# Scaling the memory rows of a two-layer decoder: four VectorE multiplications behind two powers, or four on GpSimd behind one

## The chip, the cores and the metric

The kernel runs on one core of one Trainium2 chip. The core has engines that run side by side, each with a queue of its own that it works off in order: TensorE (PE in the profile) multiplies matrices and transposes, VectorE (DVE), ScalarE (ACT) and GpSimd (POOL) do elementwise work, SyncE (SP) starts most transfers. An instruction starts when the one ahead of it on its engine is through and what it waits for is there. The metric is the device time of one execution in microseconds (us), the median of the runs; before the change 1529.76 us (three runs, 1529.23 to 1529.96).

## The reference, cut to what matters

```python
for l in range(DEPTH):                                   # 2 layers
    a = hybrid_mixer(rms_norm(x, pre_mix_g[l]), ...)     # latent + dilated attention
    x = x + rms_norm(a, post_mix_g[l])
    c = memory_cross_attention(rms_norm(x, pre_xattn_g[l]), rms_norm(mem, mem_g[l]), ...)
    x = x + rms_norm(c, post_xattn_g[l])
    x = x + rms_norm(squared_relu_mlp(rms_norm(x, pre_mlp_g[l])), post_mlp_g[l])

def rms_norm(x, g):
    return x * rsqrt(mean(x * x, axis=-1) + 1e-6) * g
```

x is 512 tokens by 1024, mem 256 memory tokens by 1024, all in float32. The change is in `rms_norm(mem, ...)`: the factor of each memory row, and the multiplication by it. The gain g is taken into the weights w_xk and w_xv.

## The kernel before

Products in float32 accuracy are made of three fast passes (lines 247 to 249): every operand is split into a rounded high part, by ScalarE (`whi`, `mth`), and a rest, by VectorE (`wlo`, `mtl`). PSUM, where TensorE writes, is cut into small pools of buffers: the pool `pst` has two buffers (tag "t") for everything that is transposed, the pool `pss` two (tag "s") for attention scores. A third tile of a pool has to wait until the first has been read out.

In the mixer, attention over 16 heads (`attention`, 8 dilated and 8 latent ones) is the main strand. `weave` fills in the latent projections (`latent`) and the keys and values of the memory (`memory`). With the 31st step of `latent`, `memory_norm` (line 829) is let in, one step of it for each step of `latent`: it loads the four 128x512 pieces of the memory (`mr`, two tiles t of 128 tokens by two halves n), takes sums of squares on ScalarE (line 381), then for each t adds the halves' sums (line 385, `nmm`), takes the power -0.5 on GpSimd (line 139, `nmr`) and multiplies the rows on VectorE (line 841). `memory` then transposes the scaled rows on TensorE (`tp<-ident,mr`, line 230), and ScalarE and VectorE split the transposed tile into `mth` and `mtl` (lines 203 and 205), from which the keys (`pfm<-mtl,whi`) are computed.

The same stretch of the program holds, of the attention: scores of latent heads (`sp<-ring`, line 481), their bias and maximum on VectorE (line 486), the exponential on ScalarE (line 490), the row factors (line 494, VectorE) and the multiplication by them on GpSimd (line 497), transposes of the probabilities (`ptp`, line 230) and their copies out of PSUM (`PT`, line 514 on VectorE, line 516 on ScalarE), and the weighted values (`op`, line 238); of the latent projections: query columns (`ptm`, then `qst`, line 767), rotary parts on GpSimd (lines 620 to 624), transposed queries (`qtp`) and keys (`pkn`), both split into `ring`, and the shared rotary key copied by GpSimd (line 802).

The order of the instructions on each engine isn't written out by hand here. A scheduler takes the program in the order in which the generators yield it, with its own idea of what is ready when, and lays out each engine's queue. So an edit of a few instructions moves others nearby.

Of the kernel before, what the change touches and what calls it, by code (L numbers as in the profile page):

```python
# [16 lines left out]
OP = mybir.AluOpType  # L17
# [15 lines left out]
EPS = 1e-6  # L33
# [12 lines left out]
def block_kernel(ctx: ExitStack, tc, x, mem, positions, rel_bias, w_in, q_norm_g, w_uq, kv_norm_g,  # L46
# [3 lines left out]
    nc = tc.nc  # L50
# [13 lines left out]
    def unit(name, shape=(128, 512), dt=F32):  # L64
        return un.tile(list(shape), dt, tag="u", name=name)

    def small(name, w):
        return sm.tile([128, 4], F32, tag="sm", name=name)[:, :w]
# [68 lines left out]
    def rpow(m, name):  # L137
        r = small(name + "r", m.shape[1])
        nc.gpsimd.tensor_tensor(r, m, mhalf[:, :m.shape[1]], op=OP.pow)
        return r  # L140
# [236 lines left out]
    def sumsq(src, ss, scale=1.0, junk=None):  # L377
        w = src.shape[-1]
        if junk is None:
            junk = unit("junk", (128, w))  # L380
        nc.scalar.activation(junk, src, AF.Square, scale=scale, accum_out=ss)

    def row_rstd(ms, tag):
        m = small(tag + "m", 1)
        nc.vector.scalar_tensor_tensor(m, ms[0], EPS, ms[1], op0=OP.add, op1=OP.add)
        return rpow(m, tag)
# [198 lines left out]
    for l in range(DEPTH):  # L585
# [241 lines left out]
        mr = [[None, None], [None, None]]  # L827

        def memory_norm():
            for t in range(2):  # L830
                for n in range(2):
                    mr[t][n] = unit("mr")
                    nc.sync.dma_start(mr[t][n], mem[0, t * 128:(t + 1) * 128, n * 512:(n + 1) * 512])
            yield
            for t in range(2):
                ms = small("mms", 2)
                for n in range(2):
                    sumsq(mr[t][n], ms[:, n:n + 1], scale=1.0 / 32.0)
                r = row_rstd((ms[:, 0:1], ms[:, 1:2]), "nm")
                for n in range(2):  # L840
                    nc.vector.tensor_scalar(mr[t][n], mr[t][n], r[:, 0:1], None, op0=OP.mult)
                yield

        def memory():
# [17 lines left out]
            for n in range(2):  # L862
                def ev_vx(t, ps, n=n):
# [6 lines left out]
                                           if SPLIT else None, 2, ev_vx, whole=True)  # L870

        latent_gen = with_at(latent(), memory_norm(), MEM_AT)
        outs = []

# [379 lines left out]
```

## Time and profile before

| what | value |
|---|---|
| median of 3 runs | 1529.76 us |
| profiled execution, its own time | 1530.0 us |
| its span, first to last instruction | 1528.2 us |
| PE busy | 1500.1 us, 98% |
| DVE busy | 981.5 us, 64% |
| ACT busy | 819.9 us, 54% |
| POOL busy | 251.0 us, 16% |
| mean granted TensorE clock | 0.994 |

The profile lists, for each engine, how long it was busy and with what. An idle time carries in brackets the instruction that ended it. Busy shares are means over the whole span; the change touches two stretches of some 37 us, one in each layer, and there the shares differ. Starts of instructions on one engine, one after the other, give the time from step to step; a listed duration reaches past the start of the next, since instructions overlap in the pipeline.

### The profile page before, as it was taken

The numbers are of one execution on the slowest core, as the hardware profiler recorded it, in microseconds if no ns is written. First come the engines' busy times: TensorE is split into PE (matmuls) and PEld (weight loads), VectorE is DVE, ScalarE is ACT, GpSimd is POOL, SyncE is SP. The second block draws the span as 40 slices with busy tenths as digits, with TensorE's granted clock in tenths as the row PEclk, the third lists the DMA queues.
The fourth block names the chain that finished last, engine by engine and source line by source line (L and its number), as shares of the span: only waits on it lengthen the run. The fifth ranks groups of instructions, "written<-read, shape, count | busy, mean of one in ns | idle before, by whom it ended". The sixth has DMA issues, their size and how long they took to land.

```text
span 1528.2 us, 21224 instructions
## 1 busy us (share of the span) xinstructions
PE 1500.1 (98%) x7861; PEld 1260.7 (82%) x7861; DVE 981.5 (64%) x1701; ACT 819.9 (54%) x1578; POOL 251.0 (16%) x438
## 2 busy tenths in 40 slices
PE   8999999999999999999999999999999999999997
PEld 6787788898898888888878877878988988888886
DVE  5556865456458668594874666654554694958668
ACT  5366755355356364554654666744454654546363
POOL 2143721021020000000011445201111100000002
PEclk9999999999999999999999999999999999999999
DMA  6423223513131505153642331253322324060535
GB/s 237 154 83 104 83 84 109 181 56 124 56 111 56 179 28 179 42 162 100 209 127 64 118 110 57 70 175 119 107 83 69 122 69 154 15 193 27 182 82 124
DMA packets 89580, 168.28 MB, mean 110 GB/s; under 512 B 6358, under 2 KB 12164, under 8 KB 89476
## 3 DMA queue, kind: packets, MB, share of 16 engines
q1 hardware_dynamic: 86436, 161.15, 32.7%
q0 software_dynamic: 2752, 5.24, 2.1%
q8 instruction: 62, 1.02, 0.3%
q10 hardware_dynamic: 288, 0.52, 0.1%
q14 instruction: 42, 0.34, 0.1%
HBM read 158.49 MB, written 11.03 MB: 111 GB/s over the span
## 4 chain that ended last, share of the span: by engine, by line
PE 83%; DVE 9%; issue 3%; ACT 2%; POOL 1%; DMA 1%; SPq 0%; DVEq 0%; POOLq 0%; ACTq 0%
PE pfm L248 12%; PE pfm L247 12%; PE pfm L249 12%; PE ptm L247 6%; PE ptm L249 6%; PE ptm L248 6%; PE sp L481 3%; PE wa L247 3%; PE wa L249 3%; PE wa L248 3%; PE op L238 3%; DVE wlo L199 3%; PE ptp L230 2%; PE wc L249 1%; PE wc L247 1%
## 5 line engine op out<-in xcount | busy, mean ns | idle before, releaser
L248 PE MATMUL pfm<-xth,wlo 128*128 128x512 f32 (+1 forms) x896 | 322.4, 360 | 0.6
L247 PE MATMUL pfm<-xtl,whi 128*128 128x512 f32 (+1 forms) x896 | 322.2, 360 | 0.0
L249 PE MATMUL pfm<-xth,whi 128*128 128x512 f32 (+1 forms) x896 | 321.6, 359 | 0.0
L199 DVE SCALAR_TENSOR_TENSOR wlo<-raw,gT,whi 128x512 fp32r<-128x512 f32 (+3 forms) x332 | 231.6, 735 | 126.0 <-ACT whi L193 123.7
L193 ACT ACTIVATE whi<-raw,gT 128x512 fp32r<-128x512 f32 (+2 forms) x324 | 209.5, 697 | 173.0 <-PE pfm L249 87.3
L248 PEld LDWEIGHTS pfm<-xth,wlo 128*128 128x128 f32 x896 | 169.2, 189 | 27.2 <-DVE wlo L199 1.6
L249 PEld LDWEIGHTS pfm<-xth,whi 128*128 128x128 f32 x896 | 169.2, 189 | 25.4 <-issue 0.5
L247 PEld LDWEIGHTS pfm<-xtl,whi 128*128 128x128 f32 x896 | 169.2, 189 | 24.8
L164 ACT ACTIVATE whi<-raw 128x1024 fp32r<-128x1024 f32 x112 | 118.2, 1060 | 130.7 <-PE pfm L249 54.1
L165 DVE TENSOR_TENSOR wlo<-raw,whi 128x1024 fp32r<-128x1024 f32 x112 | 134.9, 1221 | 39.2 <-ACT whi L164 39.2
L1075 POOL DMA_DIRECT2D raw<-in_w_down x8 | 9.8, 1230 | 596.2 <-DVE raw L1078 540.1
L247 PE MATMUL wa<-wlo,fh 128*128 128x512 f32 x240 | 93.6, 390 | 0.5 <-DVE acc L1184 0.5
L248 PE MATMUL wa<-whi,fl 128*128 128x512 f32 x240 | 93.4, 389 | 0.0
L249 PE MATMUL wa<-whi,fh 128*128 128x512 f32 x240 | 93.4, 389 | 0.0
L497 POOL TENSOR_SCALAR P<-P,rs 128x128 f32<-128x128 f32 (+3 forms) x128 | 72.3, 580 | 124.7 <-DVE rs L494 109.1
L490 ACT ACTIVATE P<-P,nm 128x128 f32<-128x128 f32 (+3 forms) x128 | 71.2, 557 | 23.9 <-DVE nm L486 23.5
L185 DVE TENSOR_TENSOR wlo<-raw,whi 128x1024 fp32r<-128x1024 f32 x32 | 39.1, 1223 | 59.4 <-ACT whi L184 58.6
L247 PE MATMUL ptm<-wlo,xth 128*128 128x512 f32 (+2 forms) x192 | 68.5, 358 | 2.6 <-DVE wlo L199 1.7
L184 ACT ACTIVATE whi<-raw 128x1024 fp32r<-128x1024 f32 x32 | 33.9, 1061 | 67.3 <-PE ptm L249 60.2
L1078 DVE TENSOR_TENSOR raw<-raw 128x1024 f32<-128x1024 f32 x56 | 68.0, 1220 | 0.2
L248 PE MATMUL ptm<-whi,xtl 128*128 128x512 f32 (+2 forms) x192 | 67.0, 349 | 0.6 <-DVE xtl L205 0.6
L249 PE MATMUL ptm<-whi,xth 128*128 128x512 f32 (+2 forms) x192 | 66.3, 347 | 0.0
(257 smaller groups left out, 3241.6 us busy)
## 6 DMA issues: line engine op xcount, KB each, us to landing
raw<-in_w_up SPq DMA_DIRECT2D x64, 512.0 KB, 4.8
raw<-in_w_down SPq DMA_DIRECT2D x64, 512.0 KB, 4.3
raw<-in_w_in SPq DMA_DIRECT2D x24, 512.0 KB, 5.5
raw<-in_w_xk SPq DMA_DIRECT2D x16, 512.0 KB, 4.8
raw<-in_w_xv SPq DMA_DIRECT2D x16, 512.0 KB, 4.0
raw<-in_w_mix_out SPq DMA_DIRECT2D x16, 512.0 KB, 4.4
raw<-in_w_xq SPq DMA_DIRECT2D x16, 512.0 KB, 6.5
raw<-in_w_xo SPq DMA_DIRECT2D x16, 512.0 KB, 3.6
```

Source lines behind the costliest of these rows:

```text
L164: nc.scalar.activation(hi, raw, AF.Copy)
L165: nc.vector.tensor_sub(lo, raw, hi.bitcast(F32))
L193: weight_parts[:] = [nc.scalar.activation(cols(hi, k, False), cols(raw, k, True), AF.Copy, scale=g).ins]
L199: nc.vector.scalar_tensor_tensor(lv, rv, g, hv, op0=OP.mult, op1=OP.subtract)
L238: nc.tensor.matmul(ps, lhsT=lhsT, rhs=rhs, start=start, stop=stop)
L247: in_order(nc.tensor.matmul(ps, lhsT=lh, rhs=rl, start=first, stop=False, skip_group_check=more))
L248: in_order(nc.tensor.matmul(ps, lhsT=ll, rhs=rh, start=False, stop=False, skip_group_check=more))
L249: in_order(nc.tensor.matmul(ps, lhsT=lh, rhs=rh, start=False, stop=last, skip_group_check=more))
L481: in_order(nc.tensor.matmul(sp[:, :L], lhsT=q[:, i * 128:(i + 1) * 128], rhs=k[:, :L], start=n == 0, stop=n == len(parts) - 1))
L490: nc.scalar.activation(Pi, Pi, AF.Exp, bias=nm[:, i:i + 1], scale=-1.0, accum_out=rs[:, i:i + 1])
L497: nc.gpsimd.tensor_scalar(Pq, Pq, rs[:, q:q + 1], 1.0, op0=OP.mult, op1=OP.mult)
L1078: nc.vector.tensor_add(tile_, tile_, more)
```

## The change

The two tiles share one `nmm` of two columns and one power of two columns. The sums of squares of both come first, in two steps of `memory_norm`, the multiplications after them, in two more, on GpSimd in place of VectorE. The memory's loads stay as they are, and no transfer is moved on SyncE's queue.

```diff
             yield
+            ms = small("mms", 4)
             for t in range(2):
-                ms = small("mms", 2)
                 for n in range(2):
-                    sumsq(mr[t][n], ms[:, n:n + 1], scale=1.0 / 32.0)
-                r = row_rstd((ms[:, 0:1], ms[:, 1:2]), "nm")
+                    sumsq(mr[t][n], ms[:, 2 * n + t:2 * n + t + 1], scale=1.0 / 32.0)
+                yield
+            m = small("nmm", 2)
+            nc.vector.scalar_tensor_tensor(m, ms[:, 0:2], EPS, ms[:, 2:4], op0=OP.add, op1=OP.add)
+            r = rpow(m, "nm")
+            for t in range(2):
                 for n in range(2):
-                    nc.vector.tensor_scalar(mr[t][n], mr[t][n], r[:, 0:1], None, op0=OP.mult)
+                    nc.gpsimd.tensor_scalar(mr[t][n], mr[t][n], r[:, t:t + 1], 1.0, op0=OP.mult, op1=OP.mult)
                 yield
```

The scheduler lays out the queues anew around it, in each layer in the same way. On TensorE, the scores of the first latent head over 384 and 512 keys (`sp`) stood inside the weighted values (`op`) before:

```order
L230 MATMUL ptp<-ident,P 128x128 x6
L238 MATMUL op<-PT,vd 64x512
L238 MATMUL op<-PT,vd 64x384
L481 MATMUL sp<-ring 128x384 x3
L481 MATMUL sp<-ring 128x512 x3
L238 MATMUL op<-PT,vd 64x384
L238 MATMUL op<-PT,vd 64x256 x2
L238 MATMUL op<-PT,vd 64x128 x2
L248 MATMUL ptm<-whi,cl 128x384
```

Now these scores are issued right behind the transposed queries, some twenty instructions earlier, and the same place reads:

```order
L230 MATMUL ptp<-ident,P 128x128 x3
L249 MATMUL ptm<-whi,ch 128x384
L230 MATMUL ptp<-ident,P 128x128 x3
L238 MATMUL op<-PT,vd 64x512
L238 MATMUL op<-PT,vd 64x384 x2
L238 MATMUL op<-PT,vd 64x256 x2
L238 MATMUL op<-PT,vd 64x128 x2
L247 MATMUL ptm<-wlo,ch 128x384
```

So the seven remaining products of the weighted values stand together. Some thirty instructions later on TensorE, behind the keys of the latent heads (`pkn`), the next scores, the transposes of the probabilities (`ptp`) and those of the second memory tile follow. Before:

```order
L249 MATMUL pkn<-ch,whi 128x512
L481 MATMUL sp<-ring 128x128 x3
L230 MATMUL ptp<-ident,P 128x128 x4
L481 MATMUL sp<-ring 128x256 x3
L230 MATMUL ptp<-ident,P 128x128 x6
L230 MATMUL tp<-ident,mr 128x128 x8
L481 MATMUL sp<-ring 128x384 x3
L481 MATMUL sp<-ring 128x512 x2
L247 MATMUL pfm<-mtl,whi 128x256
```

Now the ten transposes of the probabilities come in one piece. The last six of them are two tiles of three; they changed places, so that the first three now take the PSUM buffer that the first four have filled and that ScalarE copies out (line 516):

```order
L249 MATMUL pkn<-ch,whi 128x512
L481 MATMUL sp<-ring 128x128 x3
L481 MATMUL sp<-ring 128x256 x3
L230 MATMUL ptp<-ident,P 128x128 x10
L230 MATMUL tp<-ident,mr 128x128 x8
L481 MATMUL sp<-ring 128x384 x3
L481 MATMUL sp<-ring 128x512
L247 MATMUL pfm<-mtl,whi 128x256
```

That copy, `PT` 128x512, stands on ScalarE at this same place in the program. With the buffers' numbers (tp_2044 and tp_2053 are the two transposed halves of the first memory tile) its queue before is:

```order
L203 ACTIVATE mth_2038<-tp_2044 128x2x128
L203 ACTIVATE mth_2040<-tp_2053 128x2x128
L490 ACTIVATE P_2001,rs_2003<-P_2001,nm_2002 128x512
L203 ACTIVATE mth_2042<-tp_2053 128x2x128
L203 ACTIVATE ring_1452<-pkn_2082 64x512
L516 ACTIVATE PT_2070<-ptp_2071 128x512
L203 ACTIVATE ring_1452<-pkn_2082 64x512
```

and now, with tp_2039 and tp_2048 as the two halves:

```order
L203 ACTIVATE mth_2033<-tp_2039 128x2x128
L203 ACTIVATE ring_1452<-pkn_2077 64x512
L203 ACTIVATE mth_2035<-tp_2048 128x2x128
L490 ACTIVATE P_1996,rs_1998<-P_1996,nm_1997 128x512
L203 ACTIVATE ring_1452<-pkn_2077 64x512
L203 ACTIVATE mth_2037<-tp_2048 128x2x128
L516 ACTIVATE PT_2065<-ptp_2066 128x512
```

Both reads of the latent keys (`ring<-pkn`) now stand ahead of the copy, where one stood behind it, and the first of them stands ahead of the exponential.

## Rows read from the trace of the kernel before

**Rows 1.** The page: busy us of each engine, share of the span, instructions.
```profile
PE 1500.1 (98%) x7861; PEld 1260.7 (82%) x7861; DVE 981.5 (64%) x1701; ACT 819.9 (54%) x1578; POOL 251.0 (16%) x438
```

**Rows 2.** The page: shares of the chain that ended last, by engine.
```profile
PE 83%; DVE 9%; issue 3%; ACT 2%; POOL 1%; DMA 1%; SPq 0%; DVEq 0%; POOLq 0%; ACTq 0%
```

**Rows 3.** Busy us by stretch: the changed stretch of each layer, columns as headed.
```profile
core 0: us, PE busy (x) PEld busy (x) DVE busy (x) ACT busy (x) POOL busy (x), PEclk, DMA share, GB/s
159.00:195.50 36.50, 34.78 (x223) 28.49 (x222) 30.94 (x85) 27.05 (x71) 24.14 (x45) 1.00 0.32 102
911.00:947.50 36.50, 34.79 (x223) 28.49 (x222) 30.97 (x85) 27.05 (x71) 24.13 (x45) 1.00 0.32 102
```

**Rows 4.** Instructions on `nmr`: count, duration ns min/median/max, first and last start.
```profile
L841 DVE TENSOR_SCALAR mr<-mr,nmr x8: 480/512/540, 170.7 to 926.4; 128x512 f32<-128x512 f32 x8
L139 POOL TENSOR_TENSOR nmr<-nmm,mhalf x4: 558/559/560, 170.1 to 925.3; 128x1 f32<-128x1 f32 x4
```

**Rows 5.** GpSimd's groups by shape, whole span: count, busy us, mean ns, idle before.
```profile
L417 POOL TENSOR_SCALAR xn<-xs,n3r 128x512 f32<-128x512 f32 x16 | 11.9, 758 | 0.8
L139 POOL TENSOR_TENSOR pnr<-pnm,mhalf 128x2 f32<-128x2 f32 x2 | 1.9, 939 | 20.3 <-DVE pnm L1086 20.3
```

**Rows 6.** Timeline, GpSimd: start us, us, what, in brackets the idle before.
```profile
181.21 1.23 POOL L497 TENSOR_SCALAR P<-P,rs 128x512 f32<-128x512 f32 x1
```

**Rows 7.** Timeline, TensorE, the weighted values and the scores between them.
```profile
171.20 1.07 PE L238 MATMUL op<-PT,vd 128*64 128x512 f32 x2
...
174.26 1.07 PE L238 MATMUL op<-PT,vd 128*64 128x512 f32 x4
175.26 1.50 PE L481 MATMUL sp<-ring 96*128 96x384 f32 x6
176.69 1.51 PE L238 MATMUL op<-PT,vd 128*64 128x384 f32 x10
178.13 0.44 PE L248 MATMUL ptm<-whi,cl 128*128 128x384 f32 x1
```

**Rows 8.** Chain of waits in order of time: one head pair's weighted values undivided.
```profile
130.05 2.31 PE op L238 x16
```

**Rows 9.** Timeline, TensorE, from the first memory transposes to the memory's keys.
```profile
181.38 1.04 PE L230 MATMUL tp<-ident,mr 128*128 128x128 f32 x8
182.66 1.50 PE L481 MATMUL sp<-ring 96*128 96x384 f32 x6 [0.24 <-DVE nm L486]
184.00 0.40 PE L247 MATMUL pkn<-cl,whi 128*128 128x512 f32 x1
...
185.39 0.45 PE L481 MATMUL sp<-ring 96*128 96x128 f32 x3
...
187.19 0.84 PE L230 MATMUL ptp<-ident,P 128*128 128x128 f32 x6 [0.45 <-DVE rs L494]
188.36 1.20 PE L230 MATMUL tp<-ident,mr 128*128 128x128 f32 x8 [0.32 <-DVE PT L514]
189.31 1.24 PE L481 MATMUL sp<-ring 96*128 96x384 f32 x5
190.39 0.28 PE L247 MATMUL pfm<-mtl,whi 128*128 128x256 f32 x1
```

**Rows 10.** Timeline, ScalarE, up to the copy of the probabilities' first transposes.
```profile
185.27 0.72 ACT L490 ACTIVATE P<-P,nm 128x512 f32<-128x512 f32 x1
...
185.97 0.38 ACT L203 ACTIVATE mth<-tp 128x256 fp32r<-128x256 f32 x1
186.25 0.58 ACT L203 ACTIVATE ring<-pkn 64x512 fp32r<-64x512 f32 x1
186.73 0.58 ACT L516 ACTIVATE PT<-ptp 128x512 f32<-128x512 f32 x1
```

**Rows 11.** Timeline, VectorE, a weight's split and the second head's longest scores.
```profile
182.87 0.75 DVE L199 SCALAR_TENSOR_TENSOR wlo<-raw,gT,whi 128x512 fp32r<-128x512 f32 x1
...
184.52 0.68 DVE L486 CUSTOM_DVE_ANT_0 P<-sp,mask 128x512 f32<-128x512 f32 x1
```

## The prediction

> **What bounds the kernel.** I read the busy shares first, then the chain of waits, then the two stretches that the change touches, then the timelines in them. TensorE is busy 98% of the span [rows 1], and the chain that ended last is TensorE for 83% [rows 2]. So only what makes TensorE wait, or lets it wait less, can move the time; 2.2 us less on VectorE mean nothing by themselves. In the changed stretch of each layer TensorE is busy 34.78 of 36.5 us, at the full granted clock, VectorE 30.94, ScalarE 27.05, GpSimd 24.14 [rows 3]. TensorE has thus 1.7 us of idle time in each layer there, 3.4 in all: the most that the change could win by filling waits. VectorE has little room (85%), GpSimd 12 us. The two layers show the same numbers, so one error of mine counts twice.
>
> **The change, part by part, for one layer.**
>
> *The instructions themselves.* VectorE loses four multiplications of 0.51 us and one of two tiny additions, GpSimd loses two powers of 0.56 [rows 4] and gets one power of two columns (0.94 by the row of that shape [rows 5]) and four multiplications of 128x512, which take 0.76 where it does the same to other rows [rows 5]. GpSimd: 4 x 0.76 + 0.94 - 2 x 0.56 = 2.9 us more, against 12 us of idle time. Does TensorE wait for the scaled rows? It transposes the first of them at 181.38 [rows 9]. The first power came at 170.1 [rows 4]; the one power waits for the other tile's two sums of squares as well, and I put it at about 172; ahead of the multiplications on GpSimd now stand five rotary and key instructions, which at GpSimd's mean of 24.14 / 45 = 0.54 [rows 3] take 2.7. So the four end at about 172 + 2.7 + 0.9 + 3.0 = 178.6, nearly 3 us early. One GpSimd multiplication of this size took 1.23 in this very stretch [rows 6]; at that price they end at 180.5, still early. I take nothing, and up to 1.0 (four times 0.76 less 0.51) if the cover is gone. No transfer is moved. Behind the multiplications on GpSimd wait a rotary part and the first latent head's normalization; by the same sum they come about when they came before, with room until their transposes past 185.
>
> [...] The rows here say 0.76 to 0.51, half as long again. [...]
>
> *The weighted values in one piece.* A head pair's sixteen pieces take 2.31 undivided [rows 8]. Before, they are cut into three: 1.07, then 174.26 to 175.26, then 176.69 to 178.13, in sum 3.5 [rows 7]. The scores that stood between now go ahead, and two parts remain. The first still costs 1.07; the last seven eighths cost between 2.0 (their share of 2.31) and the 2.44 of now: 2.2, a gain of 0.2 (0 to 0.4).
>
> *The wait of the scores at 182.66* (0.24 before [rows 9]). These scores need a buffer that VectorE frees; VectorE gets there some 0.3 earlier, but two of the eight memory transposes (0.12 each, eight of them from 188.36 to 189.31) now come behind. With the gain above, I have the keys' products (`pkn`, 184.00) about 0.1 earlier in the end.
>
> *The wait of the probabilities' transposes.* This is the large term. Before, the last six began at 187.19 after a wait [rows 9]; ScalarE had copied out the first four at 186.73 [rows 10], in time. Now the next three need the buffer which that copy frees, and ahead of the copy ScalarE has, from the moment when the keys' products are done (185.39 + 0.15 until they can be read, less the 0.1: 185.45): `ring` 0.48 (from its start to the next), `mth` 0.38, the exponential 0.70 (start to start), `ring` 0.48, `mth` 0.38, the copy 0.58 [rows 10]. Together 3.0, so the copy ends at 188.4. TensorE goes on then in place of 187.19: 1.2 later. The second `ring` and `mth` need VectorE in between (it takes the rest of the first before ScalarE reads the second), which I reckon to be in time. From below: if ScalarE is ahead, the wait is the old one and with the 0.1 the term is -0.1. From above: if VectorE does one more weight split first (0.75 [rows 11]), it is 1.95.
>
> *From there to the memory's keys.* Before, 14 transposes took 187.19 to 189.31 with a wait of 0.32 inside [rows 9]: 2.1. Now the copies that they wait for are late together and the 14 come closer: 1.85, a gain of 0.3 (0 to 0.6). Then the first product of the memory's keys needs the split of the tile that is now transposed last: about 0.4 on ScalarE and 0.4 on VectorE behind the transposes and an exponential, against one score product less in front on TensorE (four in place of five before 190.39). I reckon a wait of 0.2 (0 to 0.6). The score product that is moved behind costs nothing in sum. Afterwards TensorE's order is again the old one, and it has no waits in which the delay could be made up.
>
> **Sum.** +1.2 - 0.3 + 0.2 = +1.1 us for a layer (the first two terms are in the 1.2), +2.2 for both. Bounds: -0.4 - 0.1 - 0.6 to the low side, which is -1.1, and 1.95 + 0.6, which is 2.5, to the high side. The profiled execution took 1530.0, its span 1528.2 with 1.8 around it. 1530.0 + 2.2 = 1532.2; it stands 0.24 over the median 1529.76, so against the median **1532.0**. Of a difference to before, about 0.2% (3.1 us) is what a measurement of this kernel can tell from none: 1526.7 to 1532.8 counts as the same.
>
> **The rivals.**
>
> *ScalarE keeps ahead.* The large term goes: VectorE comes sooner all along, so every exponential starts sooner, and ScalarE has the copy done in time. For it: VectorE is the fuller engine of the two in the stretch [rows 3] and loses 2.2 us. Against it: the six steps start only when the keys' products are done, and that hardly moves. Then -0.1 - 0.3 + 0, or down to -1.1: at -0.7 a layer 1528.4. If all idle time of the stretch is filled, 1529.76 - 3.4 = 1526.3, which counts as faster.
>
> *The second head's longest scores come late on VectorE.* They were done at 185.2, behind one weight split at 182.87 and one `mtl` [rows 11]; now a further weight split and a reciprocal stand between, and two scores on TensorE follow directly behind the keys' products where four transposes stood between them. If they end after TensorE has come to the second of these (about 185.7), TensorE waits there, and the exponential of rows 10 starts later by as much. Price: one weight split, 0.75 a layer, on top of the sum: 1532.0 + 1.5 = 1533.5, slower. For it: no slack in this chain is over 0.5 by my reckoning; against it: VectorE starts it earlier.
>
> *GpSimd is late.* The memory's transposes wait for the multiplications. It decides once these end after 181, over 2 us later than I reckon; then up to 1.0 a layer comes on top: 1532.0 + 2.0 = 1534.0. For it is the 1.23 of rows 6, against it the idle 12 us.
>
> That the change doesn't do what it says can't be: the new queues show it.
>
> **How the numbers follow.** The forecast case (+0.4 to +1.4 a layer, all but its top edge within 0.2%) gets 0.43, ScalarE ahead 0.25, of which 0.13 lies beyond 0.2% faster, the late scores 0.27, GpSimd late 0.05. So faster 0.13, same 0.43 + 0.12 = 0.55, slower 0.27 + 0.05 = 0.32. The likeliest case's own range is 1530.6 to 1532.6. The range that should hold 8 in 10 reaches down to 1528.0, past the middle of the first rival, and up to 1535.0, the upper bound (2 x 2.5 on top of the median is 1534.8) and past the two slower rivals; it leaves out a tenth below and somewhat less above.
>
> **What would show it.** In the profile after: four GpSimd multiplications of the memory rows of about 0.76, ended 2 us or more before the first memory transpose, which waits for none of them; the second part of the weighted values in one row of 2.2; between the fourth and the fifth of the ten transposes of probabilities a TensorE wait of nearly 2 us that the copy of line 516 ends, once in each layer; idle time on VectorE between 176 and 179. Wrong it is if that wait is under 0.7, if TensorE waits for GpSimd's rows, or if the keys' products come over 0.5 earlier or later than 184 in their layer's time.

## The result and the profile after

The changed kernel took 1537.26 us (median of four runs, 1534.93 to 1538.97), the kernel before 1529.57 (four runs, 1529.23 to 1529.96): ratio 1.0051, with an interval of 1.0039 to 1.0063. It is slower, by 7.7 us; forecast were 1532.0 and a range up to 1535.0. The profiled execution took 1534.93, its span is 1533.2, 5.0 more than before.

The busy shares hardly differ from [rows 1]: us, share of the span, instructions.

```profile
PE 1500.6 (98%) x7861; PEld 1262.3 (82%) x7861; DVE 979.4 (64%) x1691; ACT 820.6 (54%) x1578; POOL 255.4 (17%) x444
```

TensorE has the same 7861 instructions; it is busy 0.5 us longer and idle 4.5 us longer. TensorE's timeline of the changed kernel, at the place of [rows 9], shows where (start, duration, what, in brackets the idle time before and what ended it):

```profile
182.72 0.40 PE L247 MATMUL pkn<-cl,whi 128*128 128x512 f32 x1
...
184.11 0.91 PE L481 MATMUL sp<-ring 96*128 96x128 f32 x6
184.86 0.60 PE L230 MATMUL ptp<-ident,P 128*128 128x128 f32 x4
187.50 0.87 PE L230 MATMUL ptp<-ident,P 128*128 128x128 f32 x6 [2.04 <-ACT PT L516]
188.96 1.97 PE L230 MATMUL tp<-ident,mr 128*128 128x128 f32 x8 [0.58 <-ACT PT L516]
190.57 1.71 PE L481 MATMUL sp<-ring 96*128 96x384 f32 x4
...
195.90 0.36 PE L247 MATMUL pfm<-mtl,whi 128*128 128x256 f32 x1
```

The same in layer 1:

```profile
943.56 0.87 PE L230 MATMUL ptp<-ident,P 128*128 128x128 f32 x6 [2.05 <-ACT PT L516]
945.02 1.09 PE L230 MATMUL tp<-ident,mr 128*128 128x128 f32 x8 [0.58 <-ACT PT L516]
945.87 1.00 PE L481 MATMUL sp<-ring 96*128 96x384 f32 x4
...
950.49 0.36 PE L247 MATMUL pfm<-mtl,whi 128*128 128x256 f32 x1
```

After the first four transposes TensorE stands still for 2.04 us, and for another 0.58 before the memory's transposes; before it was 0.45 and 0.32 [rows 9]. ScalarE's timeline at that place names the reason (answers to [rows 10]):

```profile
184.37 0.59 ACT L203 ACTIVATE ring<-pkn 64x512 fp32r<-64x512 f32 x1 [0.28 <-PE pkn L249]
184.86 0.37 ACT L203 ACTIVATE mth<-tp 128x256 fp32r<-128x256 f32 x1
185.13 0.71 ACT L490 ACTIVATE P<-P,nm 128x512 f32<-128x512 f32 x1
...
185.96 0.59 ACT L203 ACTIVATE ring<-pkn 64x512 fp32r<-64x512 f32 x1
186.58 0.38 ACT L203 ACTIVATE mth<-tp 128x256 fp32r<-128x256 f32 x1
186.86 0.59 ACT L516 ACTIVATE PT<-ptp 128x512 f32<-128x512 f32 x1
```

The four transposes were done at 185.46. The copy that frees their buffer stands behind an exponential, a `ring` and an `mth`, and ends at 187.45; TensorE goes on 0.05 later.

The two layers have the same waits and not the same loss. In layer 0 the eight memory transposes take 1.97 and the four score products 1.71, in layer 1 1.09 and 1.00. The difference is the granted clock. The stretches of layer 0 (busy times, then `PEclk`, the granted share of full speed):

```profile
185.00:188.00 3.00, 0.96 (x10) 0.72 (x9) 2.96 (x6) 2.40 (x6) 2.50 (x4) 1.00 0.03 10
188.00:190.00 2.00, 1.42 (x9) 1.18 (x8) 1.25 (x6) 0.99 (x3) 0.00 (x0) 0.68 0.83 258
190.00:192.00 2.00, 2.00 (x9) 2.00 (x8) 0.50 (x2) 1.51 (x5) 0.00 (x0) 0.50 0.04 12
192.00:194.00 2.00, 2.00 (x11) 1.12 (x10) 1.83 (x6) 0.98 (x3) 1.06 (x2) 0.97 0.00 0
```

Behind the wait TensorE runs at 0.50 of full speed for some 3 us. In layer 1 of this execution the clock stays at 1.00 (937 to 952 us).

As a measure I take the time on TensorE from the first keys' product (182.72) to the fifth product of the memory's keys (195.90): 13.18 us in layer 0, 938.78 to 950.49 or 11.71 in layer 1. Before it is 9.93 (184.00 in [rows 9], and the row below) and 9.92 (936.03 to 945.95).

```profile
193.93 0.36 PE L247 MATMUL pfm<-mtl,whi 128*128 128x256 f32 x1
```

So 3.25 + 1.79 = 5.04 us more, and the span grew by 5.0. The rest of the two executions differs too, but nearly cancels. At 85 to 95 us the clock fell in both, for a shorter time in the changed kernel's execution (`PEclk` 0.97 and 0.69 in the halves of this stretch, 0.80 and 0.52 before), and TensorE was 1.3 us ahead from there on; at 770 to 780 it fell for a longer time (0.74 and 0.58, before 0.66 and 1.00), which took back 0.8, and 0.3 more went at 998.

### The profile page after: what moved, and what is told of

It is laid out like the page before. It is cut to its first block, busy times and chain, and to the rows that moved or that the text cites. A ratio compares the mean times of both kernels' runs of the same rounds, so it can differ in the third digit from the quotient of the medians.

```text
span 1533.2 us, 21228 instructions
## 1 busy us (share of the span) xinstructions
PE 1500.6 (98%) x7861; PEld 1262.3 (82%) x7861; DVE 979.4 (64%) x1691; ACT 820.6 (54%) x1578; POOL 255.4 (17%) x444
## 3 DMA queue, kind: packets, MB, share of 16 engines
q8 instruction: 62, 1.02, 0.3%
## 4 chain that ended last, share of the span: by engine, by line
PE 84%; DVE 8%; ACT 3%; issue 2%; POOL 1%; DMA 0%; SPq 0%; DVEq 0%; POOLq 0%; ACTq 0%
PE pfm L248 12%; PE pfm L247 12%; PE pfm L249 12%; PE ptm L247 7%; PE ptm L249 7%; PE ptm L248 7%; PE sp L481 3%; PE wa L247 3%; PE wa L248 3%; PE wa L249 3%; PE op L238 3%; DVE wlo L199 2%; PE ptp L230 2%; PE wc L248 1%; PE wc L249 1%
```

## The experiments

The theory: the change's own instructions cost nothing; the scheduler puts ScalarE's copy behind other work, TensorE waits for it, and behind the wait the clock falls in most executions. The first rival: scaling on GpSimd, or the wait for both tiles, costs by itself. The second: TensorE's changed order costs. The third, on the clock: it falls by chance, whatever TensorE does.

All times are medians of five or more executions beside runs of the kernel before on the same chip (1530.29, 1529.99, 1529.66 and 1529.98 in the four sets, at least 21 each; single ones 1527.4 to 1532.3); a ratio is one of means, so it can differ a little from that of the medians. The stretch of 9.93 us above, in the profiled execution of each kernel (waits: the last six transposes of probabilities, and the memory's transposes):

| kernel | time | ratio, interval | layer 0, layer 1 | waits |
|---|---|---|---|---|
| changed, again | 1537.97 | 1.0053 [1.0041, 1.0065] | 13.24, 14.47 | 2.06, 0.58 |
| GpSimd, two powers | 1536.07 | 1.0033 [1.0021, 1.0045] | 13.17, 13.00 | 1.98, 0.58 |
| one power, VectorE | 1531.39 | 1.0007 [0.9999, 1.0016] | another order | 0, 0.33 |
| one read held back | 1533.45 | 1.0019 [1.0010, 1.0028] | 10.84, 10.83 | 1.01 + 0.34, 0 |
| exponential held back | 1536.28 | 1.0035 [1.0023, 1.0048] | 11.45, 12.74 | 1.81, 0.58 |
| both held back | 1531.66 | 1.0008 [0.9999, 1.0016] | 10.51, 10.51 | 0.75 + 0.31, 0 |
| six transposes repeated | 1535.24 | 1.0032 [1.0020, 1.0045] | 13.22, 11.70 | 1.40, 0.58 |
| twelve repeated | 1531.12 | 1.0011 [1.0002, 1.0020] | 10.43, 10.43 (holds 1.00 of work less) | 0.80, 0.38 |

### Which half of the change

The changed kernel once more:

> The changed kernel once more, for a second profile and for how far its runs lie apart. Theory (queue order): in each layer TensorE waits about 2.0 us between the fourth and the fifth of the ten transposes of probabilities, until ScalarE's copy of line 516; that is +4.0 for both layers, the same in every execution, 1534 with nothing else. What a run takes beyond that is half-speed clock behind these waits: a profile above 1535 shows the granted clock at 0.5 in one or both of the two stretches, one below none or one. Rival: the waits themselves differ from run to run; then a slower profile shows waits over 2.3 us at a full clock. Median 1535 to 1539.

1537.97 (1536.85 to 1538.95). In its profile the clock fell in both layers, and in layer 1 for longer:

```profile
190.00:192.00 2.00, 2.00 (x10) 2.00 (x11) 0.60 (x3) 1.35 (x6) 0.00 (x0) 0.50 0.39 146
192.00:194.00 2.00, 2.00 (x11) 1.90 (x10) 1.17 (x4) 1.10 (x4) 0.61 (x1) 0.71 0.00 0
...
945.00:948.00 3.00, 2.89 (x12) 2.89 (x13) 0.74 (x3) 2.02 (x8) 0.00 (x0) 0.50 0.37 140
948.00:952.00 4.00, 4.00 (x14) 2.35 (x13) 2.45 (x8) 1.61 (x5) 1.83 (x4) 0.63 0.00 0
```

So one and the same wait costs 1.79 us with the full clock (layer 1 of the first profile), 3.3 with a short fall and 4.55 (14.47 less 9.92) with a longer one. The span is 8.0 longer than before, 3.31 + 4.55 of it in the two stretches.

GpSimd scales, with a power for each tile:

```diff
# of the kernel before
-                    nc.vector.tensor_scalar(mr[t][n], mr[t][n], r[:, 0:1], None, op0=OP.mult)
+                    nc.gpsimd.tensor_scalar(mr[t][n], mr[t][n], r[:, 0:1], 1.0, op0=OP.mult, op1=OP.mult)
```

> Only one part of the change: the memory rows are multiplied on GpSimd, but with one power for each token tile as before. Its ScalarE queue at the critical place is that of the change (ring, mth, exponential, ring, mth, copy). Theory (queue order): the wait before the fifth transpose is there again, 1.8 to 2.2 us in each layer; 1534 to 1538. Rival (the single power makes the rows or the sums late): without it the time goes back to 1529 to 1531.

1536.07, with the waits of the changed kernel. Its executions lie far apart and follow the mean granted clock: 1531.70 at 0.998, 1533.15 at 0.997, 1534.78 at 0.996, 1536.07 at 0.995, 1536.38 at 0.994, 1536.79 at 0.992, 1538.87 at 0.991.

One power for both tiles, VectorE scales:

```diff
# of the changed kernel
-                    nc.gpsimd.tensor_scalar(mr[t][n], mr[t][n], r[:, t:t + 1], 1.0, op0=OP.mult, op1=OP.mult)
+                    nc.vector.tensor_scalar(mr[t][n], mr[t][n], r[:, t:t + 1], None, op0=OP.mult)
```

> Only the other part: one power for both token tiles, but the multiplications stay on VectorE. In its ScalarE queue the copy of line 516 stands ahead of the exponential and of the second read of the keys. Theory (queue order): the wait before the fifth transpose is under 0.8 us; 1528.5 to 1531.5, no difference to before. Rival (the two sums of squares and the single power behind them are what costs): 1533 or more.

1531.39: the interval holds no change. The copy stands ahead of the exponential here (188.05 and 188.53), and the last six transposes don't wait. The GpSimd half makes the loss; whether by its instructions or by the queues that come with it, this pair doesn't tell.

### What stands ahead of the copy

Three kernels change the queue around the copy. TensorE's order is that of the changed kernel, in the first up to the memory's keys, in the other two in all 7861 instructions. In the first, one read of the keys' product and its split wait until the copy is issued:

```diff
# of the changed kernel, in keys_values; shortened
-                        split_from(k[0][0:NOPE, :], k[1][0:NOPE, :], ps[e * 64:(e + 1) * 64, :])
+                        if n == 1 and m == 0 and e == 1:
+                            held_keys.append(keyed_in)   # the same split_from, under tc.issue_after(copied)
```

> The changed kernel with the second read of the latent keys on ScalarE (and its rest on VectorE) queued behind the copy of line 516; TensorE's order is the same up to the memory's keys. ScalarE reaches the copy one read and one split earlier, 0.9 us by the change's profile. Theory (queue order): the wait before the fifth transpose falls from 2.04 to about 1.1 in each layer, the time by 1.8 or more: 1531 to 1534. Rival (another thing, VectorE or the buffer of the other tile, is late just behind it): the wait moves to the next transposes and the time stays at 1535 to 1538.

1533.45; a stretch costs 0.91 in place of 1.79, and the clock stayed at 1.00 there in the profiled execution. The median lies 3.2 above the kernel before, the two stretches hold 1.8 of it; the mean clocks of its executions, 0.992 to 0.997, leave room for falls in others.

In the second, the long exponential stands behind the copy:

```diff
# of the changed kernel, in scores; shortened
+            behind_copy = held[0] if held and i == 3 else last_key[0] if pinned[0] and i == 0 else None
+            with tc.issue_after(behind_copy) if behind_copy is not None else nullcontext():
                 nc.scalar.activation(Pi, Pi, AF.Exp, bias=nm[:, i:i + 1], scale=-1.0, accum_out=rs[:, i:i + 1])
```

> The changed kernel with one thing moved: the exponential of the long row (128x512, 0.70 us from start to start) stands behind the copy of the first four transposes, in both layers; every row on TensorE stays where it was. Theory (TensorE waits for what stands ahead of that copy on ScalarE): the wait of 2.05 us falls to about 1.4, the cost of a stretch before any loss of clock from 2.0 to about 1.4, and the time to 1532.7 if TensorE keeps its full clock behind the wait and up to 1536 if it does not. Rival (the order of TensorE itself, which is the same here as in the changed kernel, costs the time): no change against the changed kernel, 1537 to 1538.

1536.28, and a wait of 1.81 where 1.4 was expected. ScalarE's rows show why:

```profile
183.18 0.59 ACT L203 ACTIVATE ring<-pkn 64x512 fp32r<-64x512 f32 x1 [0.29 <-PE pkn L249]
183.67 0.37 ACT L203 ACTIVATE mth<-tp 128x256 fp32r<-128x256 f32 x1
184.52 0.59 ACT L203 ACTIVATE ring<-pkn 64x512 fp32r<-64x512 f32 x1 [0.48 <-DVE ring L205]
185.14 0.38 ACT L203 ACTIVATE mth<-tp 128x256 fp32r<-128x256 f32 x1
185.42 0.59 ACT L520 ACTIVATE PT<-ptp 128x512 f32<-128x512 f32 x1
```

The second `ring` now waits 0.48 for VectorE, which the exponential had covered. So the size was missed. The fastest execution, at a mean clock of 0.998, took 1532.16, the others (0.992 to 0.995) 1534.6 to 1537.3. That fastest one is the profiled one: even in it the clock fell behind layer 1's wait (12.74, against 11.45 in layer 0), but not at 85 to 95 and at 770 us, where it fell before.

In the third both edits are made:

> As the run before, and the second read of the keys' product with its split (0.48 us on ScalarE) stands behind the copy as well; TensorE's rows again all where they were. Theory: the wait falls to about 0.7 us, with up to 0.4 more where the next three transposes wait for VectorE's split; a stretch costs 0.5 to 0.9 in place of 2.0, the granted clock stays at 1.00 behind the wait, and the time is 1531.0 to 1531.8. Rival (TensorE's own order): 1537 to 1538.

1531.66 (1529.47 to 1532.66), and 10.51 in both layers. ScalarE now waits for the first four transposes and copies them at once. The next three still wait 0.75 for the copy, the last three 0.31 for VectorE; TensorE's waits are down from 2.62 to 1.06:

```profile
185.95 0.60 ACT L520 ACTIVATE PT<-ptp 128x512 f32<-128x512 f32 x1 [0.32 <-PE ptp L230]
```

```profile
185.25 0.60 PE L230 MATMUL ptp<-ident,P 128*128 128x128 f32 x4
186.60 0.55 PE L230 MATMUL ptp<-ident,P 128*128 128x128 f32 x3 [0.75 <-ACT PT L520]
187.46 0.55 PE L230 MATMUL ptp<-ident,P 128*128 128x128 f32 x3 [0.31 <-DVE mtl L205]
```

With GpSimd's four multiplications still there and TensorE's order unchanged, 6.0 of the 7.7 us are gone, each counted from the kernel before beside it. Both first rivals fall as causes of the loss; the interval doesn't tell the 1.7 that are left from nothing.

### The clock

TensorE repeats six of the four transposes just made, same data, same buffer, inside its wait:

```diff
# of the changed kernel, in transposed_scores, for the first latent head
+                if again and b == 0:
+                    for n in range(AGAIN):          # 6, and 12 in the second kernel
+                        i = n % 4
+                        in_order(nc.tensor.transpose(tp[:, i * 128:i * 128 + 128], P[:, OFFS[i]:OFFS[i] + 128], ident))
```

> The changed kernel, in which TensorE repeats, right behind the first four transposes and into the same buffer with the same data, six of them (0.12 us each, 0.7 in all): work that changes nothing and lies inside the wait of 2.05 us. All other rows of all engines stay in order. If it is the idle time that lets the clock fall: the transposes behind come no earlier and no later, the wait reads 1.35, the granted clock stays at 1.00 from there on, and the time is that of before plus the bare wait, 1530.1 + 4.1 = 1534.2. If the clock falls all the same, or if no part of the loss is the clock's: 1537 to 1538, as the changed kernel.

1535.24: between the two forecasts. Two of five executions kept 0.997 or 0.998 and took 1533.85 and 1533.13; three had 0.994 and took 1535.2 to 1536.6. In the profiled one the clock fell in layer 0 (13.22) and not in layer 1 (11.70, within 0.01 of the 11.71 that the changed kernel took at the full clock). So behind waits of 1.40 and 0.58 the clock still fell in one of the two places.

> As the run with six repeated transposes, with twelve: 1.4 us of the wait of 2.05 are filled. One long row of scores on TensorE stands some rows later than in the changed kernel, otherwise the order is the same. If the idle time lets the clock fall, it stays at 1.00 behind the wait in nearly every execution and the time is before plus the bare wait: 1532.5 to 1534.2, with less spread than the run with six (1533.1 to 1536.6). If the fall comes from something else than idle time: as that run, 1535 to 1537.

1531.12, in eleven executions with a spread of 2.3 us. No fall in the two stretches of the profiled one, and the time is 1.4 to 3.1 under what I expected. TensorE's order differs here: a row of scores stands later, and the next weighted values are in one piece. These are eight products, each of two instructions. In the changed kernel as in the one before, the first product goes alone, then the rest; here all sixteen instructions stand together. The layer-0 timelines, twelve repeated first, then the kernel before:

```profile
195.77 2.37 PE L238 MATMUL op<-PT,vm 128*64 128x512 f32 x16
198.07 0.39 PE L247 MATMUL pfm<-mtl,whi 128*128 128x256 f32 x1
```

```profile
191.43 1.07 PE L238 MATMUL op<-PT,vm 128*64 128x512 f32 x2
192.43 0.39 PE L247 MATMUL pfm<-mtl,whi 128*128 128x256 f32 x1
...
195.86 2.37 PE L238 MATMUL op<-PT,vm 128*64 128x512 f32 x14
198.16 0.39 PE L247 MATMUL pfm<-mtl,whi 128*128 128x256 f32 x1
```

Sixteen take 2.30 to the next start, and so do the fourteen that are left when two have run before for 1.00. The 10.43 of the table lack these 1.00, so the stretch costs 1.5 more than before, and the gain of 1.0 a layer hides most of that. This run shows the clock (in its profile it no longer falls behind the wait), not the price of the wait.

For the clock alone, the kernel before has places of its own: at 85 to 95 us and at 770 its clock falls. Idle products (of a matrix of zeros, with a result that nobody reads) in its waits there, nothing else moved:

```diff
# of the kernel before
+            if pinned[0] and not scores_begun[0] and i in (1, 2):   # in scores, first head
+                idle_products(8)
...
+                    if l < DEPTH - 1:                               # behind the last products of layer 0
+                        idle_products(8)
```

> The kernel before, with idle products (0.11 us each) in two places where it already waits: eight behind the second and eight behind the third scores of the first head, at 86 and 88 us (waits of 1.01 and 0.94), and eight around the first transposes of the second layer's rows at 767 to 770 us (waits of 1.05 and 0.43). Nothing else moves. If idle time lets the clock fall, the 6.8 us at half clock behind 88 us and the 3.4 at 771 go, which gives back up to 3.4 and 1.7: 1525.0 to 1528.0. If the idle products only cost (up to 0.2 at each place) and the clock falls anyway: 1530 to 1531.

> The kernel before with the idle products once more, to narrow the interval: 1528.5, under the kernel before by 1.0 to 1.8 us, in executions whose granted clock is 0.997 to 0.999. If the first comparison was chance: 1529.5 to 1530.

1528.54 and 1528.90, ratios 0.9992 [0.9983, 1.0001] and 0.9993 [0.9984, 1.0001]. Before, then with the idle products:

```profile
85.00:90.00 5.00, 2.90 (x11) 2.19 (x12) 4.10 (x13) 4.92 (x11) 2.83 (x3) 0.80 0.66 157
90.00:95.00 5.00, 5.00 (x22) 4.74 (x21) 3.29 (x12) 2.88 (x12) 2.92 (x8) 0.52 0.64 200
770.00:775.00 5.00, 4.19 (x16) 3.37 (x17) 4.92 (x10) 4.48 (x10) 1.45 (x3) 0.66 0.57 201
```

```profile
85.00:90.00 5.00, 4.60 (x30) 3.47 (x31) 4.59 (x13) 4.92 (x11) 3.04 (x3) 1.00 0.52 156
90.00:95.00 5.00, 4.43 (x33) 4.10 (x32) 3.34 (x15) 3.75 (x14) 3.31 (x10) 1.00 0.66 212
770.00:775.00 5.00, 4.78 (x22) 3.26 (x21) 5.00 (x9) 4.23 (x10) 1.68 (x2) 1.00 0.42 118
```

All three stretches are at 1.00 now. One profile each could be chance, but there are seventeen, of all the kernels here: of the twelve without these idle products ten show a fall at 87 to 95 us and nine one at 769 to 780, of the five with them none. And where TensorE waits 1.40 to 2.06 us for the copy, the clock fell behind it in 10 of 14 places; in the same stretch of the kernels where it waits 1.02 or less for it, in 1 of 20. So here it is the idle time that lets the clock fall, and the third rival is out.

The gain in time is 0.8 to 1.5 us, less than the 2 to 5 expected; each interval just reaches no change. The profiles show where it went. From 85 to 95 us TensorE gains 2.1 in both. At 770 it gains nothing: from the transposes at 771.25 to those at 782.98 it takes 11.73 before, and 11.72 and 11.73 with the idle products (769.22 to 780.94 and 768.95 to 780.68). VectorE is busy for 17.44 of the 18.00 us from 766 to 784 there, and TensorE, sooner at its products, now waits 0.22 and 0.18 for it.

### Whole weighted values, with and without the change

```diff
# of each kernel, in weighted_values
         for j in range(NT):                          # shortened
-            for e in range(2):
+            for e in ((1, 0) if j == 0 else (0, 1)):
+                with tc.issue_after(second) if (j, e) == (0, 0) else nullcontext():   # second: the product of e = 1
```

> The kernel before, with the sixteen products of the weighted values of each head pair kept in one piece (the first product of the second head now stands ahead of the first of the first head, and TensorE's queue cannot pull one of them forward). Before, two of the eight are cut in each layer: into three pieces of 1.07, 1.0 and 1.4 at 171 to 178 us, and into 1.07 and 2.30 at 191 to 198 us; an uncut one takes 2.30. If a first product alone costs its full 1.07 and the rest takes as long as the whole, 1.2 and 1.05 fall away in each layer: 1529.9 less 4.5, 1525.4. If the pieces only filled waits that then show: 1529 to 1530.

1537.94, ratio 1.0052 [1.0040, 1.0064], where 1525.4 was expected. This miss shows the cause without the change. The scheduler answered to this edit, too, with the copy behind the exponential (188.08), the second `ring` and `mth`; the kernel holds nothing of the change, and has its waits to 0.01:

```profile
188.91 0.59 ACT L203 ACTIVATE ring<-pkn 64x512 fp32r<-64x512 f32 x1
189.53 0.38 ACT L203 ACTIVATE mth<-tp 128x256 fp32r<-128x256 f32 x1
189.81 0.59 ACT L516 ACTIVATE PT<-ptp 128x512 f32<-128x512 f32 x1
```

```profile
187.80 0.60 PE L230 MATMUL ptp<-ident,P 128*128 128x128 f32 x4
190.46 1.34 PE L230 MATMUL ptp<-ident,P 128*128 128x128 f32 x6 [2.05 <-ACT PT L516]
192.38 1.92 PE L230 MATMUL tp<-ident,mr 128*128 128x128 f32 x8 [0.58 <-ACT PT L516]
```

Waits of 1.08 and 0.75 at 171 us came on top, which the pieces had filled, with a clock of 0.61 behind them in layer 0 (173 to 176 us), and one head pair is still cut in each layer (four instructions, then twelve). The stretches take 12.06 and 13.39, 5.6 of the 8.0 us by which the span grew. That the total equals the changed kernel's is thus chance; that the waits do is not.

> The changed kernel with the same. Its queues come out differently around the change: the copy of the first four transposes stands on ScalarE ahead of the second read of the keys' product, behind the long row's exponential. If the change's own instructions cost nothing and only the queue order did: within 1.5 us of the kernel before with uncut products, 1525 to 1527. If the changed instructions cost by themselves, wherever the copy stands: 5 to 8 us over that kernel, 1530 to 1533.

1530.63, 7.3 less than the same without the change. The number lies where the rival had put it, but the rival was 5 to 8 us over the kernel without the change, and that one came out as slow as said. Here the scheduler left the copy ahead of the second read, and no wait there is over 0.7. Whether the scaling is on VectorE or on GpSimd doesn't decide. In this pair TensorE's order went along with the copy's place; the kernel with both held back, above, parts the two, and there the copy's place decides.

> The kernel before with uncut products and with the idle products at 86, 88 and 767 us. If both gains stand: 1525.4 less 1.2, 1524.2. If they overlap: 1525.4.

1535.52 for both edits on the kernel before, over both forecasts like the kernel that it is made from: the idle products keep the clock up at 85 to 95 us and do nothing for the late copy.

> The changed kernel with both pieces of ScalarE's work behind the copy and with the idle products at 86, 88 and 767 us. The two add up if they are separate: 1531.7 less 1.5, 1530.2 (1529.5 to 1531). If the gain of the idle products depends on the state of the queues around the change: 1531 to 1532.

1530.25: the kernel with both held back and with the idle products gets the two gains added, as expected.

> The changed kernel with uncut products, with both pieces of ScalarE's work behind the copy, and with the idle products. With 0.6 a stretch left of the change's cost: 1524.2 + 1.2, 1525.4; if the uncut products need the order that this one changes: 1527 or more.

1527.21 (1526.75 to 1529.19), ratio 0.9985 [0.9976, 0.9994], the second of the two forecasts: the changed kernel with the copy first, whole weighted values and the idle products beats both kernels. Its TensorE is busy 1496.9 us, 3.2 less than before [rows 1].

## Why the prediction was wrong

*GpSimd's rows cost nothing:* right. The four multiplications took 2.71 together, 0.68 each (0.76 expected), and ended at 175.4, the power took 0.71; the first memory transpose came at 180.03 and waited for none of them. GpSimd's timeline after:

```profile
171.43 0.71 POOL L139 TENSOR_TENSOR nmr<-nmm,mhalf 128x2 f32<-128x2 f32 x1
...
172.70 2.71 POOL L845 TENSOR_SCALAR mr<-mr,nmr 128x512 f32<-128x512 f32 x4
```

The rival with GpSimd late falls with 4.6 us to spare. The single instruction is longer on GpSimd, 0.68 against 0.51 on VectorE [rows 4]; that decided nothing.

*The weighted values in one piece, -0.2:* about right. The second part took 2.29 from its start to the next (174.83 to 177.12) where 2.44 stood before, a gain of 0.15; 2.2 were reckoned. Nothing of it, nor of the 0.1 reckoned for the keys' products, was left at these: in layer 1 they came 2.75 later than before, and so did the weighted values at 905 us, ahead of the change. In layer 0 they came at 182.72, over 0.5 earlier than 184, which the prediction named as a sign of being wrong; it is none, as TensorE had been 1.3 ahead since 95 us.

*The wait of the probabilities' transposes, +1.2:* the mechanism was right in every link (ScalarE's order, the buffer, the place, both layers), also against the rival in which ScalarE keeps ahead. The chain from the first `ring` to the copy's end took 3.08 where 3.0 were reckoned. That is partly luck: the two `mth` took 0.27 and 0.28 where 0.38 were taken, the exponential and the second `ring` 0.83 and 0.62 where 0.70 and 0.48 were. From the keys' products to the last six transposes it is 4.78 in layer 1 (943.56 less 938.78) against 3.19 before, so +1.6.

*From there to the memory's keys, -0.1:* +0.2. I expected the late transposes to close up. But the second copy can begin only when the late transposes are through, so the wait of 0.32 grew to 0.58. Together the two terms make 1.79 a layer in place of 1.1, which by itself would have given 1529.76 + 3.58 = 1533.3, within the range.

*The step that failed:* "at the full granted clock". I took the 1.00 of [rows 3] as given also for the time behind the new wait and priced that wait in TensorE's idle time alone; the sum has no term for the clock. Of the changed kernel's 7.7 us 2 x 1.79 = 3.6 are waiting. The 4.1 that are left I put down to the clock, whose price the profile taken again shows: 1.5 in layer 0 and 2.8 in layer 1, 4.3 together. The trace of before held the warning: waits of 1.01 and 0.94 for the first scores at 86 to 89 us, and behind them 0.52 in the stretch 90 to 95. TensorE had not stood still all the time ahead of the fall in the changed kernel: it was busy 0.96 of the 3.0 us from 185 to 188.

The second rival (VectorE late with the long scores) didn't occur: these ran on VectorE at 183.68, and the scores at 184.11 waited for nothing:

```profile
183.68 0.65 DVE L486 CUSTOM_DVE_ANT_0 P<-sp,mask 128x512 f32<-128x512 f32 x1
```

Not settled: why the fall comes in one execution and layer and not in the other, with the same wait to 0.01 us; and why the medians of the kernel before with idle products lie only 0.8 to 1.5 lower, where its profiles gained 2.1.

## What to carry to other kernels

Where a scheduler lays out the queues, an edit's price is mostly that of the order which comes with it: follow each copy that frees a PSUM buffer and ask what has come to stand ahead of it; here two instructions of ScalarE held behind it were worth 6 us. Price a wait of TensorE twice, once as idle time (here 1.79 us a layer) and once as the clock behind it (here 1.5 and 2.8), from places in the trace where it waited as long. And compare an edit with the same edit under a fixed order before it is kept or dropped: an unrelated edit brought the same waits and a loss as large.

## What the hardware showed beside that

The weighted values are products that write 64 of 128 partitions, and the two heads of a pair write the two halves. The products of the two heads overlap: the first product alone, 512 wide, takes 1.00 us, and at that price the eight together, 2560 wide, would take 5.0 one after the other (an estimate); they take 2.30 to the next start. The second piece of [rows 7] shows it for two: one head's product, 512 wide, and the other's, 384 wide, take 1.00 together (174.26 to 175.26). If the first head's first product goes alone for 1.00, the rest takes 2.30 all the same, since the other head's four are still whole. So the piece that goes alone at 191 us costs its 1.00 on top, while the pieces at 171 us filled waits, of 1.08 and 0.75 in the kernel before with whole weighted values.
